# A two-layer decoder trunk on one core: where attention's and the mixer's small transposes stand in TensorE's queue

## The chip, the cores and the metric

The kernel runs on one core of one Trainium2 chip. The metric is the device time of one execution in microseconds (us), lower is better. The kernel before takes 1362.99 us, the median of three runs (1362.9 to 1364.49).

The engines named here are TensorE (PE, matrix products and transposes), VectorE (DVE), ScalarE (ACT), GpSimd (POOL) and the queue that starts most loads (SP). TensorE writes into PSUM banks; DVE and ACT read them from there.

## The reference

The program is a trunk of two layers over 512 tokens with 1024 channels, in float32:

```python
# layer 0
x = x + mamba2_mixer(x)      # 4 groups; per group: y = rms_norm(y_group) ; then y @ out_w
x = x + conv_ffn(x)
# layer 1
k, v = shared_kv(x)          # k = rms_norm per 64 channels
q = rms_norm(rms_norm(x) @ q_w)
logits = q @ k.T * scale + bias[t5_bucket(distance)]        # causal, two maps a head
attn = softmax(logits[0]) - lam * softmax(logits[1])
o = rms_norm(attn @ v) * (1 - lam_init)                      # 8 heads of 128 channels
x = x + o @ out_w
x = x + conv_ffn(x)
```

Three things in it matter here. The mixer's result is normed group by group (512 channels each) before its output projection. Keys and queries are normed after their projection. Each head's result `o` is normed over its 128 channels before the output projection, in which every one of the eight heads takes part.

## The kernel before

**Products.** Activations lie with channels on the partitions, as `xT[0..7]`, eight blocks of 128 channels by 512 tokens. Every large product is done as three passes (`mm3`, L195): high part by high part, high by low, low by high. So one block of 128 output channels over eight input blocks is 24 products of 128x128 by 128x512, and over four input blocks it is 12. Each chunk of weights is loaded by SP into a raw buffer (three), and split by ACT (`wh`, L147 or L165) and DVE (`wl`, L151 or L166) into one of three weight buffers. `chunk()` (L187) starts the loads and splits two chunks ahead of the use. Of the eight PSUM banks four are for products (`mm_bank`) and four for everything else (`aux_bank`).

**Order.** The order on each engine isn't the program's order. A planner goes through the instructions by priority, which is the place in the program, and puts each where, by its own estimate of durations, its inputs are ready. If an instruction isn't ready by that estimate, a later one that is ready goes ahead. On the chip each engine then takes its instructions in that fixed order, and waits where one isn't ready yet. `tc.issue_after(ins)` gives every instruction traced inside it, on the engine of `ins`, one more condition for the planner: it comes behind `ins`. It is no wait on the chip.

**Mixer.** For each of four groups: two blocks of products and convolutions for B and C (`conv_block`, L528), four for the values, then the scan woven with four blocks for the gate. Then the sum of squares over the group's channels (`gacc`) is turned into a factor for each token: `token_rsqrt` (L443) transposes the sums (`tr_g`, L447), reduces them and takes the inverse root by twelve small DVE instructions (L418 to L430), and `along_tokens` (L453) transposes the factor back into a row (`al_g`, L457). `normed` (L740) does both and then makes the normed high and low parts `yh`, `yl`. They are read by `out_proj` (L700), eight blocks of 12 products: for group g it comes at the end of group g + 1. In the last group three blocks of `out_proj(2)` come ahead of `normed`, and five behind it.

**Attention.** `proj` (L917) makes keys, queries or values of four heads, in four pieces of 24 products, and yields after each half piece (12 products). `qk` (L939) adds the norm over 64 channels (ACT L945 and L946, DVE L947, the inverse root, DVE L954) and turns the normed tokens by sixteen transposes (`ktk`, `ktq`, L958) into `kT` and `qT`. The position biases are a product of a small one-hot table (`ps_rb`, L907), written to DRAM (`bd`, L911) and read back per head (`tr`, L986) for the logits.

Each head has three parts of query blocks, and each part goes through four steps: `logits` (L981, products `lg` L1001, DVE L1007, exponentials L1015), `weigh` (L1018), `turn` (transposes `at`, L1033) and `values` (products `po`, L1042, copied by ACT to `ot`, L1045). `heads` (L1066) runs the steps of successive parts one round apart. When a head's last part is through, `finish` (L1048) norms it (ACT L1052, DVE L1053, inverse root, DVE L1055 on `ot`), turns it by four transposes (`oT`, L1058), and makes the high and low parts `oh` (ACT L1061) and `ol` (DVE L1062).

The heads are woven with other products: heads 0 to 3 with the value projection (`lead_in`, L464) and then with the next keys and queries (`weave`, L472, one half piece for two steps); heads 4 to 7 with their values and then with the first half of the output projection, `attn_out(0)`, one block for four steps. `attn_out(1)` follows at the end: for each of the eight blocks of output channels 12 products over heads 4 to 7 (`ps_ao`), then `add_to_stream` (L511): DVE adds the block to `xT` (L512), ACT scales the high part `xgh` (L414), DVE makes the low part `xgl` (L415), ACT squares and POOL adds (L498, L500). The first product group of the second FFN (`ps_g`) reads all eight `xgh` and `xgl`, one after the other.

Of the kernel before, what the change touches and what calls it, by code (L numbers as in the profile page):

```python
# [18 lines left out]
P = 128  # L19
# [20 lines left out]
def trunk_kernel(ctx: ExitStack, tc, x, ssm_ln_g, ssm_in_w, ssm_conv_w, ssm_conv_b, ssm_dt_bias,  # L40
# [154 lines left out]
    def mm3(ps, wh, wl, xh, xl, start, stop):  # L195
        pe.matmul(ps, wh, xh, start=start, stop=False)  # L196
        pe.matmul(ps, wh, xl, start=False, stop=False)  # L197
        pe.matmul(ps, wl, xh, start=False, stop=stop)  # L198
# [319 lines left out]
    with tc.tile_pool(name="ssm_y", bufs=1) as yp, tc.tile_pool(name="ssm", bufs=1) as sp:  # L518
        def in_block(key):
# [4 lines left out]
            for k in range(KB):  # L524
                mm3(ps, wh[:, k, :], wl[:, k, :], xgh[k], xgl[k], k == 0, k == KB - 1)
# [174 lines left out]
        def out_proj(g, yh, yl, norm):  # L700
            for c in range(4):
                wh, wl = chunk("out%d_%d" % (g, c))
                for i in range(2):
                    m = 2 * c + i
                    ps = mm_bank("ps_o%d_%d" % (g, m))
                    for k in range(4):
                        mm3(ps, wh[:, k, i * P:(i + 1) * P], wl[:, k, i * P:(i + 1) * P],
                            yh[k], yl[k], k == 0, k == 3)
# [31 lines left out]
        def normed(g, xs, acc):  # L740
            r = along_tokens(token_rsqrt(acc, sp, "g%d" % g, 512), "g%d" % g)
# [14 lines left out]
        for g in range(NG):  # L756
# [6 lines left out]
            conv_block(16 + g, "in%d" % (32 + g), bT)  # L763
            conv_block(20 + g, "in%d" % (36 + g), cT)
# [10 lines left out]
            for b in range(4):  # L775
# [5 lines left out]
                else:  # L781
                    a2 = sp.tile([P, T], F32, tag="gacc", name="gacc%d_%d" % (g, b), bufs=2)
                    (pool if b == 1 else dve).tensor_tensor(out=a2, in0=acc, in1=sq, op=ALU.add)
                    acc = a2
            if g == 0:
                params_b()
                prev = normed(g, xs, acc)
            elif g < NG - 1:
                run(out_proj(g - 1, *prev, None))
                prev = normed(g, xs, acc)  # L790
            else:
# [3 lines left out]
                prev = normed(g, xs, acc)  # L795
# [99 lines left out]
    with tc.tile_pool(name="att_o", bufs=1) as op_, tc.tile_pool(name="att", bufs=1) as ap:  # L895
        rts = []

# [3 lines left out]
        hb = NBIAS // 2  # L901
        for i in range(2):
            oh = ap.tile([32, hb], F32, tag="p0", name="oh%d" % i, bufs=3)
            bv = ap.tile([AH, hb], F32, tag="p1", name="bv%d" % i, bufs=3)
            sync.dma_start(oh, onehot[:, i * hb:(i + 1) * hb])
            ps = aux_bank("ps_rb%d" % i)
            pe.matmul(ps[:AH, :hb], rb, oh, start=True, stop=True)  # L907
            act.activation(bv, ps[:AH, :hb], AF.Copy)
            if i == 0:
                dve.memset(bv[:, 0:P - 1], NEG)  # L910
            sync.dma_start(bd[:, i * hb:(i + 1) * hb], bv)  # L911
# [5 lines left out]
        def proj(key, evac):  # L917
            pss = [mm_bank("ps_%s_%d" % (key, b)) for b in range(NT)]
            for k0 in range(0, KB, 2):
                wh, wl = chunk("%s_%d" % (key, k0))  # L920
                for b in range(NT):
                    ts = slice(b * P, (b + 1) * P)
                    for k in range(k0, k0 + 2):
# [3 lines left out]
                        pe.matmul(pss[b], xgl[k][:, ts], wh[:, k - k0, :], start=False, stop=sp_)  # L927
                    if b == 1:
                        yield
# [9 lines left out]
        def qk(key, dst, gcol):  # L939
# [12 lines left out]
            for b in range(NT):  # L952
# [3 lines left out]
                ps = aux_bank("kt%s_%d" % (key, b))  # L956
                for h in range(4):
                    pe.transpose(ps[:, h * P:(h + 1) * P], kn[b][:, h * P:(h + 1) * P], ident)  # L958
                act.activation(dst[:, :, b * P:(b + 1) * P], ps.rearrange("p (h t) -> p h t", h=4),
                               AF.Copy, scale=c2[:, gcol:gcol + 1])  # L960
# [87 lines left out]
        def finish(h, st):  # L1048
# [6 lines left out]
            dve.tensor_tensor(out=ot, in0=ot, in1=so.unsqueeze(2).to_broadcast([P, NT, P]), op=ALU.mult)  # L1055
            ps = aux_bank("oT%d" % h)
# [9 lines left out]
        def heads(hs, os):  # L1066
# [6 lines left out]
            for t in range(n + 4):  # L1073
                if t < n:
                    us[t].logits()
                    yield
# [8 lines left out]
                if 0 <= t - 4 < n and us[t - 4].part == len(PARTS) - 1:  # L1085
                    os.append(finish(us[t - 4].h, us[t - 4].st))
                    yield

        def attn_out(i, os, norm):
            for c in range(4):  # L1090
                wh, wl = chunk("ao%d_%d" % (i, c))
                for j in range(2):
                    m = 2 * c + j
                    ps = mm_bank("ps_ao%d_%d" % (i, m))
                    for k in range(4):
                        mm3(ps, wh[:, k, j * P:(j + 1) * P], wl[:, k, j * P:(j + 1) * P],
                            os[k][0], os[k][1], k == 0, k == 3)
                    add_to_stream(m, ps, 24, norm)
# [48 lines left out]
```

## Time and profile before

| | before |
|---|---|
| median of 3 runs | 1362.99 us (1362.9 to 1364.49) |
| the profiled execution | 1362.61 us |
| its span, from the first to the last instruction | 1360.5 us |
| granted TensorE clock, mean | 0.999 |
| PE busy | 1349.6 us (99%) |
| DVE, ACT, POOL busy | 912.9, 664.5, 90.8 us |
| the mixer's groups | until about 384 us of the span |
| attention, from the first key product to the last of the output projection | 744.4 to 992.3 us |

The view of the profile that counts most here is that of the waits: for each kind of instruction it sums the time that its engine stood idle ahead of it, and names what ended the idle time. The time rows give one instruction each: its start in us from the begin of the span, its duration, engine, line, operation, output and inputs, shapes and count; in brackets the idle time ahead of it and what ended it. PE's products are pipelined: the 512-column products start 0.23 us apart and are shown as 0.39 long. So a row with no bracket may still start late against the row ahead.

### The profile page before, as it was taken

To read this page: it belongs to the slowest core of one execution; us is meant where nothing else is said; L and a number is where in the kernel's file an instruction comes from. 1 tells how busy PE (TensorE), PEld (TensorE's weight loads), DVE (VectorE), ACT (ScalarE), POOL (GpSimd) and SP (SyncE) were. 2 spreads that over 40 slices of the span, in tenths; PEclk is the share of its full clock that TensorE was granted. 3 is DMA by queue.
4 is the path that set the end of the run, shared out by engine and by line. 5 is a ranking of instruction groups with operands and counts; after the bars stand their busy time and mean duration, and the time that the engine had idled before them with its cause. 6 is when DMAs were issued, how large, how long until landed. Compare 5 with 4: busy or idle time off the path is not lost.

```text
span 1360.5 us, 16900 instructions
## 1 busy us (share of the span) xinstructions
PE 1349.6 (99%) x6421; PEld 1096.7 (81%) x6421; DVE 912.9 (67%) x1528; ACT 664.5 (49%) x1090; POOL 90.8 (7%) x118
## 2 busy tenths in 40 slices
PE   9999999999999999999999999999999999999998
PEld 7878887887888888888888777777788888888887
DVE  5989778688877774367755565767777773367742
ACT  5696744652444443134434466777664443134420
POOL 4330301200010000000002000000110000000000
PEclk9999999999999999999999999999999999999999
DMA  7452433432333332333233332221223333333322
GB/s 202 144 163 78 147 109 95 146 93 70 93 93 93 95 107 93 93 95 105 88 93 104 117 86 70 78 78 56 58 82 93 96 105 94 93 96 105 94 93 78
DMA packets 179904, 135.06 MB, mean 99 GB/s; under 512 B 6508, under 2 KB 163632, under 8 KB 179824
## 3 DMA queue, kind: packets, MB, share of 16 engines
q1 hardware_dynamic: 174048, 120.84, 30.0%
q0 software_dynamic: 4496, 12.05, 2.8%
q10 hardware_dynamic: 1280, 1.10, 0.2%
q8 instruction: 50, 0.82, 0.2%
q14 instruction: 30, 0.25, 0.1%
HBM read 131.72 MB, written 2.25 MB: 98 GB/s over the span
## 4 chain that ended last, share of the span: by engine, by line
PE 90%; DVE 5%; ACT 3%; issue 1%; DMA 1%; SPq 0%; DVEq 0%; ACTq 0%
PE ps_g L197 6%; PE ps_g L198 6%; PE ps_g L196 6%; PE ps_u L196 6%; PE ps_u L198 6%; PE ps_u L197 6%; PE ps_in L197 5%; PE ps_in L198 5%; PE ps_in L196 5%; PE ps_d L848 3%; PE ps_d L196 3%; PE ps_d L198 3%; PE ps_d L847 3%; PE ps_d L846 3%; PE ps_d L197 3%; PE ps_o L198 2%
## 5 line engine op out<-in xcount | busy, mean ns | idle before, releaser
L196 PE MATMUL ps_u<-xgh,wh_u 128*128 128x512 f32 x352 | 137.5, 391 | 0.0
L197 PE MATMUL ps_g<-xgl,wh_g 128*128 128x512 f32 x352 | 137.1, 390 | 0.0
L196 PE MATMUL ps_g<-xgh,wh_g 128*128 128x512 f32 x352 | 137.1, 390 | 0.0
L198 PE MATMUL ps_u<-xgh,wl_u 128*128 128x512 f32 x352 | 137.1, 389 | 0.0
L198 PE MATMUL ps_g<-xgh,wl_g 128*128 128x512 f32 x352 | 137.1, 389 | 0.0
L197 PE MATMUL ps_u<-xgl,wh_u 128*128 128x512 f32 x352 | 137.1, 389 | 0.0
L197 PE MATMUL ps_in<-xgl,wh_in 128*128 128x512 f32 x304 | 121.0, 398 | 0.0
L196 PE MATMUL ps_in<-xgh,wh_in 128*128 128x512 f32 x304 | 120.9, 398 | 0.0
L198 PE MATMUL ps_in<-xgh,wl_in 128*128 128x512 f32 x304 | 119.6, 394 | 0.0
L151 DVE TENSOR_TENSOR wl_d<-wr_d,wh_d 128x1024 fp32r<-128x1024 f32 (+1 forms) x46 | 54.2, 1179 | 96.9 <-ACT wh_d L147 96.7
L147 ACT ACTIVATE wh_d<-wr_d 128x1024 fp32r<-128x1024 f32 (+1 forms) x46 | 47.1, 1024 | 130.3 <-PE ps_d L848 62.4
L870 ACT ACTIVATE hh<-vg 128x512 fp32r<-128x512 f32 x44 | 27.8, 632 | 114.9 <-DVE vg L869 114.9
L818 DVE TENSOR_TENSOR uu<-ps_u,nr_f 128x512 f32<-128x512 f32 x44 | 30.4, 692 | 78.0 <-PE ps_u L198 77.9
L197 PEld LDWEIGHTS ps_g<-xgl,wh_g 128*128 128x128 f32 x352 | 66.1, 188 | 13.9 <-DVE xgl L415 0.3
L198 PEld LDWEIGHTS ps_u<-xgh,wl_u 128*128 128x128 f32 x352 | 66.1, 188 | 13.8
L198 PEld LDWEIGHTS ps_g<-xgh,wl_g 128*128 128x128 f32 x352 | 66.1, 188 | 13.7
L196 PEld LDWEIGHTS ps_g<-xgh,wh_g 128*128 128x128 f32 x352 | 66.1, 188 | 13.6
L197 PEld LDWEIGHTS ps_u<-xgl,wh_u 128*128 128x128 f32 x352 | 66.1, 188 | 13.6
L196 PEld LDWEIGHTS ps_u<-xgh,wh_u 128*128 128x128 f32 x352 | 66.1, 188 | 13.5
L147 ACT ACTIVATE wh_g<-wr_g 128x1024 fp32r<-128x1024 f32 x44 | 46.7, 1061 | 51.7 <-PE ps_u L197 32.3
L865 ACT ACTIVATE vg<-vg 128x512 f32<-128x512 f32 x44 | 27.8, 632 | 84.4 <-DVE vg L821 84.4
L846 PE MATMUL ps_d<-wh_d,hh 128*128 128x512 f32 x176 | 68.5, 389 | 0.0
(349 smaller groups left out, 3228.3 us busy)
## 6 DMA issues: line engine op xcount, KB each, us to landing
wr_g<-in_ffn_up_w_dram SPq DMA_DIRECT2D x44, 512.0 KB, 3.9
wr_u<-in_ffn_up_w_dram SPq DMA_DIRECT2D x44, 512.0 KB, 3.9
wr_d<-in_ffn_down_w_dram SPq DMA_DIRECT2D x42, 512.0 KB, 3.6
wr_in<-in_ssm_in_w_dram SPq DMA_DIRECT2D x40, 512.0 KB, 3.9
m<-cumd POOLq DMA_DIRECT2D x16, 512.0 KB, 4.5
wr_out<-in_ssm_out_w_dram SPq DMA_DIRECT2D x16, 512.0 KB, 3.5
wr_k<-in_kv_w_dram SPq DMA_DIRECT2D x8, 512.0 KB, 4.0
wr_q<-in_q_w_dram SPq DMA_DIRECT2D x8, 512.0 KB, 4.1
```

Of the source, the lines that this page charges most:

```text
L147: return act.activation(self.wh[:, :self.n], self.raw[:, :self.n], AF.Copy)
L151: return dve.tensor_tensor(out=self.wl[:, :self.n], in0=self.raw[:, :self.n], in1=self.wh[:, :self.n].bitcast(F32), op=ALU.subtract)
L196: pe.matmul(ps, wh, xh, start=start, stop=False)
L197: pe.matmul(ps, wh, xl, start=False, stop=False)
L198: pe.matmul(ps, wl, xh, start=False, stop=stop)
L818: dve.tensor_tensor(out=u, in0=ps, in1=r, op=ALU.mult)
L846: pe.matmul(pss[b], hh[k][:, ts], wh[:, k - k0, :], start=k == 0, stop=False)
L847: pe.matmul(pss[b], hh[k][:, ts], wl[:, k - k0, :], start=False, stop=False)
L848: pe.matmul(pss[b], hl[k][:, ts], wh[:, k - k0, :], start=False, stop=k == n - 1)
L865: act.activation(ga, ga, AF.Silu)
L870: act.activation(h, ga, AF.Copy)
```

## The change

Five edits, which share one device: `mm3` returns its last product, and `state["last"]` holds the last large product that was traced.

- The mixer: the factor is computed where it was, but `along_tokens` and the normed parts come behind the first convolution block of the next group (24 products), and are put behind its last product. In the last group they come two blocks of `out_proj(2)` later, behind the fifth of eight.
- Attention gets a list `pend`. What is on it is traced at the next call of `pended()`, behind `state["last"]`. Such calls stand in `proj` after the first half of each piece, at the head of each round of `heads`, and in the last output projection.
- The transposes of keys and queries (`turned`), and those of the normed head with `oh` and `ol` (`turned_out`), are put on that list; the norm itself stays where it was.
- The bias rows are put on the list after the fourth half piece of `k0`, and so come behind its 60th product; the one-hot table's loads stay first.
- The first half piece of each value projection is traced ahead of the heads that it is woven with, so that the queries' transposes have products to stand behind. The weave of the heads with the other products is thereby shifted by one half piece.
- `attn_out(1)` does the first five blocks (m0 to m4) in two goes: nine products over heads 4 to 6 first, the three over head 7 later. Head 7's transposes come behind the nine products of m3. Then come nine of m4, the three last ones of m0 to m4 with their additions, and m5 to m7 as before. The block m4 has a bank of the other four.

```diff
         pe.matmul(ps, wh, xl, start=False, stop=False)
-        pe.matmul(ps, wl, xh, start=False, stop=stop)
+        return pe.matmul(ps, wl, xh, start=False, stop=stop).ins
...
             for k in range(KB):
-                mm3(ps, wh[:, k, :], wl[:, k, :], xgh[k], xgl[k], k == 0, k == KB - 1)
+                state["last"] = mm3(ps, wh[:, k, :], wl[:, k, :], xgh[k], xgl[k], k == 0, k == KB - 1)
             return ps
...
                     for k in range(4):
-                        mm3(ps, wh[:, k, i * P:(i + 1) * P], wl[:, k, i * P:(i + 1) * P],
-                            yh[k], yl[k], k == 0, k == 3)
+                        state["last"] = mm3(ps, wh[:, k, i * P:(i + 1) * P], wl[:, k, i * P:(i + 1) * P],
+                                            yh[k], yl[k], k == 0, k == 3)
                     add_to_stream(m, ps, 16, norm)
...
-        def normed(g, xs, acc):
-            r = along_tokens(token_rsqrt(acc, sp, "g%d" % g, 512), "g%d" % g)
+        def normed(g, xs, rt):
+            with tc.issue_after(state["last"]):
+                r = along_tokens(rt, "g%d" % g)
             yh, yl = [], []
...
             conv_block(16 + g, "in%d" % (32 + g), bT)
+            if g:
+                prev = normed(*todo)
             conv_block(20 + g, "in%d" % (36 + g), cT)
...
                     acc = a2
+            factor = lambda: token_rsqrt(acc, sp, "g%d" % g, 512)
             if g == 0:
                 params_b()
-                prev = normed(g, xs, acc)
+                todo = g, xs, factor()
             elif g < NG - 1:
                 run(out_proj(g - 1, *prev, None))
-                prev = normed(g, xs, acc)
+                todo = g, xs, factor()
             else:
...
                     next(op)
-                prev = normed(g, xs, acc)
+                rt = factor()
+                for _ in range(2):
+                    next(op)
+                prev = normed(g, xs, rt)
                 run(op)
...
         rts = []
+        pend = []
+        def pended():
+            with tc.issue_after(state["last"]):
+                for f in pend:
+                    f()
+            pend.clear()
...
         hb = NBIAS // 2
+        ohs = []
         for i in range(2):
-            oh = ap.tile([32, hb], F32, tag="p0", name="oh%d" % i, bufs=3)
-            bv = ap.tile([AH, hb], F32, tag="p1", name="bv%d" % i, bufs=3)
-            sync.dma_start(oh, onehot[:, i * hb:(i + 1) * hb])
-            ps = aux_bank("ps_rb%d" % i)
-            pe.matmul(ps[:AH, :hb], rb, oh, start=True, stop=True)
-            act.activation(bv, ps[:AH, :hb], AF.Copy)
-            if i == 0:
-                dve.memset(bv[:, 0:P - 1], NEG)
-            sync.dma_start(bd[:, i * hb:(i + 1) * hb], bv)
+            ohs.append(ap.tile([32, hb], F32, tag="p0", name="oh%d" % i, bufs=3))
+            sync.dma_start(ohs[i], onehot[:, i * hb:(i + 1) * hb])
+        def bias_rows():
+            for i in range(2):
+                bv = ap.tile([AH, hb], F32, tag="p1", name="bv%d" % i, bufs=3)
+                ps = aux_bank("ps_rb%d" % i)
+                pe.matmul(ps[:AH, :hb], rb, ohs[i], start=True, stop=True)
+                act.activation(bv, ps[:AH, :hb], AF.Copy)
+                if i == 0:
+                    dve.memset(bv[:, 0:P - 1], NEG)
+                sync.dma_start(bd[:, i * hb:(i + 1) * hb], bv)
...
                         pe.matmul(pss[b], xgh[k][:, ts], wl[:, k - k0, :], start=False, stop=False)
-                        pe.matmul(pss[b], xgl[k][:, ts], wh[:, k - k0, :], start=False, stop=sp_)
+                        state["last"] = pe.matmul(pss[b], xgl[k][:, ts], wh[:, k - k0, :],
+                                                  start=False, stop=sp_).ins
                     if b == 1:
+                        pended()
                         yield
...
                                   op=ALU.mult)
-                ps = aux_bank("kt%s_%d" % (key, b))
-                for h in range(4):
-                    pe.transpose(ps[:, h * P:(h + 1) * P], kn[b][:, h * P:(h + 1) * P], ident)
-                act.activation(dst[:, :, b * P:(b + 1) * P], ps.rearrange("p (h t) -> p h t", h=4),
-                               AF.Copy, scale=c2[:, gcol:gcol + 1])
+            def turned():
+                for b in range(NT):
+                    ps = aux_bank("kt%s_%d" % (key, b))
+                    for h in range(4):
+                        pe.transpose(ps[:, h * P:(h + 1) * P], kn[b][:, h * P:(h + 1) * P], ident)
+                    act.activation(dst[:, :, b * P:(b + 1) * P], ps.rearrange("p (h t) -> p h t", h=4),
+                                   AF.Copy, scale=c2[:, gcol:gcol + 1])
+            pend.append(turned)
             yield
...
-        def finish(h, st):
+        def normed_out(h, st):
             ot = st["ot"]
...
             dve.tensor_tensor(out=ot, in0=ot, in1=so.unsqueeze(2).to_broadcast([P, NT, P]), op=ALU.mult)
+        def turned_out(h, st):
+            ot = st["ot"]
             ps = aux_bank("oT%d" % h)
...
             for t in range(n + 4):
+                pended()
                 if t < n:
...
                 if 0 <= t - 4 < n and us[t - 4].part == len(PARTS) - 1:
-                    os.append(finish(us[t - 4].h, us[t - 4].st))
+                    normed_out(us[t - 4].h, us[t - 4].st)
+                    pend.append(lambda u=us[t - 4]: os.append(turned_out(u.h, u.st)))
                     yield
...
         def attn_out(i, os, norm):
+            held = []
             for c in range(4):
                 wh, wl = chunk("ao%d_%d" % (i, c))
-                for j in range(2):
-                    m = 2 * c + j
-                    ps = mm_bank("ps_ao%d_%d" % (i, m))
-                    for k in range(4):
-                        mm3(ps, wh[:, k, j * P:(j + 1) * P], wl[:, k, j * P:(j + 1) * P],
-                            os[k][0], os[k][1], k == 0, k == 3)
-                    add_to_stream(m, ps, 24, norm)
-                    yield
-        run(qk("k0", kT[0], 48))
-        run(qk("q0", qT[0], 49))
+                late = (2, 2, 1, 0)[c] if i else 0
+                pss = [(aux_bank if c == 2 and j < late else mm_bank)("ps_ao%d_%d" % (i, 2 * c + j))
+                       for j in range(2)]
+                def part(j, ks, c=c, wh=wh, wl=wl, pss=pss):
+                    for k in ks:
+                        state["last"] = mm3(pss[j], wh[:, k, j * P:(j + 1) * P], wl[:, k, j * P:(j + 1) * P],
+                                            os[k][0], os[k][1], k == 0, k == 3)
+                    if 3 in ks:
+                        add_to_stream(2 * c + j, pss[j], 24, norm)
+                        yield
+                for j in range(late):
+                    run(part(j, range(3)))
+                    held.append(part(j, (3,)))
+                if late and c == 1:
+                    pended()
+                if c == 2:
+                    yield from chain(*held)
+                for j in range(late, 2):
+                    yield from part(j, range(4))
+        ops = chain(qk("k0", kT[0], 48), qk("q0", qT[0], 49))
+        for _ in range(4):
+            next(ops)
+        pend.append(bias_rows)
+        run(ops)
         os0, os1 = [], []
-        lead_in(hs := heads(range(0, 4), os0), vproj("v0", 0), 2)
+        next(vp := vproj("v0", 0))
+        lead_in(hs := heads(range(0, 4), os0), vp, 2)
         weave(hs, chain(qk("k1", kT[1], 48), qk("q1", qT[1], 49)), 1, 2)
-        lead_in(hs := heads(range(4, 8), os1), vproj("v1", 1), 2)
+        next(vp := vproj("v1", 1))
+        lead_in(hs := heads(range(4, 8), os1), vp, 2)
         weave(hs, attn_out(0, os0, None), 1, 4)
```

## The prediction

> **What bounds the kernel now.** I read the page first, then the waits of TensorE (PE), then the time rows round each wait that an edit touches.
>
> ```profile
> PE 1349.6 (99%) x6421; PEld 1096.7 (81%) x6421; DVE 912.9 (67%) x1528; ACT 664.5 (49%) x1090; POOL 90.8 (7%) x118
> PE 90%; DVE 5%; ACT 3%; issue 1%; DMA 1%; SPq 0%; DVEq 0%; ACTq 0%
> ```
>
> PE is busy for 99% of the span and carries 90% of the chain that ended last. No product is removed, so the change can only win what PE waits, and a refill behind each wait. The view of waits, for PE alone, in us in total, times and longest:
>
> ```profile
> PE oT L1058 <- DVE ot L1055: 3.1, 5, 1.1
> ...
> PE al_g L457 <- DVE tr_g L430: 0.6, 2, 0.3
> ...
> PE ktk L958 <- DVE knk L954: 0.3, 1, 0.3
> PE ps_rb L907 <- DMA oh<-onehot_dram: 0.3, 1, 0.3
> ...
> PE ktq L958 <- DVE knq L954: 0.2, 1, 0.2
> ```
>
> The edits aim at these 4.5 us in ten waits. Each waiting instruction is a small transpose or product, and PE takes matmuls in the order of its queue, so the big products behind it stand too.
>
> **1. The mixer's factor rows (al_g).** Time rows of PE round the wait in group 1:
>
> ```profile
> 178.27 0.40 PE L198 MATMUL ps_o<-yh,wl_out 128*128 128x512 f32 x1
> 178.50 0.38 PE L447 MATMUL tr_g<-ident,gacc 128*128 128x128 f32 x2
> ...
> 182.83 0.39 PE L198 MATMUL ps_in<-xgh,wl_in 128*128 128x512 f32 x1
> 183.53 0.62 PE L457 MATMUL al_g<-ident,tr_g 128*128 128x128 f32 x4 [0.32 <-DVE tr_g L430]
> ```
>
> Without a wait a transpose starts 0.23 us behind the product ahead of it (178.27 to 178.50); here it took 0.70. So a wait costs its idle time and about 0.16 us more, 0.48 in all. The chain of DVE behind tr_g lasts 5.0 us (178.50 to 183.53). Now al_g stands behind all 24 products of the next group's first block, 24 x 0.23 = 5.4 us, after four tr_g transposes (0.36, an estimate from two in 0.38 with overlap): it starts at 5.8, and 0.8 us are to spare. Two such waits (the row gives 0.6 in 2): gain **0.95**. If DVE were later by more than 0.8, it would come back. The normed tiles are read by a projection a whole group later, so their delay of about 0.8 us reaches nobody. In the last group two more blocks of products stand ahead of it; no wait is listed there, and I count nothing.
>
> **2. The bias rows (ps_rb).**
>
> ```profile
> 744.36 0.39 PE L925 MATMUL ps_k<-wh_k,xgh 128*128 128x512 f32 x1
> ...
> 747.76 0.39 PE L925 MATMUL ps_k<-wh_k,xgh 128*128 128x512 f32 x1
> 748.40 1.23 PE L907 MATMUL ps_rb<-oh,rb 32*8 32x320 f32 x4 [0.25 <-DMA oh<-onehot_dram]
> ...
> 800.60 1.80 PE L1001 MATMUL lg<-kT,qT 64*128 64x128 f32 x12
> ```
>
> From 747.76 to 748.40 are 0.64, against 0.23: 0.41. Behind 60 products of k0 instead of 16 the four matmuls run at about 744.4 + 13.6 = 758.0, and the DMA has long landed. The two writes of bd on SP and the reads of tr behind them move by about 10 us; their first user, logits, is at 800.60, so 30 us hide them. The weight loads queued behind them on SP are fetched two chunks ahead. Gain **0.41**.
>
> **3. Keys, queries, heads 0 to 6.** A transpose put "behind a later product" has only a lower bound: the planner places an instruction where it holds it ready, and it did so before.
>
> ```profile
> 768.30 0.39 PE L925 MATMUL ps_q<-wh_q,xgh 128*128 128x512 f32 x1
> ...
> 773.51 0.39 PE L927 MATMUL ps_q<-wh_q,xgl 128*128 128x512 f32 x1
> 773.97 0.66 PE L958 MATMUL ktk<-ident,knk 128*128 128x128 f32 x4
> ```
>
> The keys already stand behind 24 products of q0 (768.30 to 773.51 is 5.2 us); the new bound is 12, so it binds nothing. The heads:
>
> ```profile
> 927.83 1.06 PE L1042 MATMUL po<-vt,at 128*128 128x128 f32 x8
> ...
> 931.58 0.93 PE L1001 MATMUL lg<-kT,qT 64*128 64x128 f32 x8
> ...
> 933.41 0.48 PE L196 MATMUL ps_ao<-oh,wh_ao 128*128 128x512 f32 x1
> ...
> 936.48 0.39 PE L197 MATMUL ps_ao<-ol,wh_ao 128*128 128x512 f32 x1
> 937.80 0.41 PE L1058 MATMUL oT<-ident,ot 128*128 128x128 f32 x2 [0.93 <-DVE ot L1055]
> ...
> 954.91 0.41 PE L1058 MATMUL oT<-ident,ot 128*128 128x128 f32 x2 [1.07 <-DVE ot L1055]
> ...
> 967.08 0.41 PE L1058 MATMUL oT<-ident,ot 128*128 128x128 f32 x2 [0.66 <-DVE ot L1055]
> ```
>
> From 933.41 to 936.48 lie 14 products: all of block m2 and two of m3, and then oT of head 4 waits 0.93. The new bound is "behind m2", which the old order meets. Heads 5 and 6 are alike (bounds m4 and m7). With head 3 (3.1 less these three and head 7's 0.18 leaves about 0.23), the keys (0.3, and 0.07 at 773.97) and the queries (0.2) these are seven waits of 3.5 us idle, 4.6 with 0.16 for each. They can all go, because every step of the weave is shifted by half a step; or none, since the placing by readiness stays. I hold the second as nearer, as the rows show the bound met already, and count one wait in seven as lost by the shift: gain **0.65**, ends 0 and 4.6 (the other end is rival C).
>
> **4. The last head.** Rows of ACT, PE and DVE:
>
> ```profile
> 970.16 0.28 ACT L1045 ACTIVATE ot<-po 128x128 f32<-128x128 f32 x1 [1.04 <-PE po L1042]
> ...
> 973.39 0.39 PE L198 MATMUL ps_ao<-oh,wl_ao 128*128 128x512 f32 x1
> 973.96 0.63 PE L1058 MATMUL oT<-ident,ot 128*128 128x128 f32 x4 [0.18 <-DVE ot L1055]
> ...
> 975.35 0.75 DVE L1062 SCALAR_TENSOR_TENSOR ol<-oT,c,oh 128x512 fp32r<-128x512 f32 x1 [1.54 <-ACT oh L1061]
> ```
>
> The chain from 970.16 to the transpose is 3.8 us; 36 products of blocks m0 to m3 (8.2 us) now cover it. From the transpose's start to the end of ol are 2.1 us; four transposes (0.4) and nine products of m4 (2.0) cover that by 0.3. Gain 0.57 - 0.23 = **0.34**.
>
> Its price lies behind it. Five blocks now end within 15 products (3.4 us), and all additions come late. Groups of DVE instructions from the first addition to the last low part, and the rows at both ends:
>
> ```profile
> L415 DVE SCALAR_TENSOR_TENSOR xgl<-xT,c,xgh 128x512 fp32r<-128x512 f32 x8 | 7.9, 1005 | 1.6 <-ACT xgh L414 1.6
> L512 DVE TENSOR_TENSOR xT<-ps_ao,xT 128x512 f32<-128x512 f32 x8 | 5.4, 684 | 1.0 <-PE ps_ao L198 0.9
> L151 DVE TENSOR_TENSOR wl_g<-wr_g,wh_g 128x1024 fp32r<-128x1024 f32 x2 | 2.8, 1386 | 0.3 <-ACT wh_g L147 0.2
> L151 DVE TENSOR_TENSOR wl_u<-wr_u,wh_u 128x1024 fp32r<-128x1024 f32 x1 | 1.5, 1536 | 0.1
> L151 DVE TENSOR_TENSOR wl_ao<-wr_ao,wh_ao 128x1024 fp32r<-128x1024 f32 x1 | 1.2, 1226 | 0.0
> ```
> ```profile
> 977.04 1.29 DVE L512 TENSOR_TENSOR xT<-ps_ao,xT 128x512 f32<-128x512 f32 x2 [0.94 <-PE ps_ao L198]
> ...
> 992.26 0.39 PE L196 MATMUL ps_g<-xgh,wh_g 128*128 128x512 f32 x1
> ...
> 997.26 0.50 PE L197 MATMUL ps_g<-xgl,wh_g 128*128 128x512 f32 x1
> ```
>
> Call S the first product of the FFN (992.26). PE asks for the last xgl at S + 5.0 (997.26); its row is long, so it came just in time. DVE began at S - 15.2 and had 20.2 us. In the new order the first block ends 48 products ahead of S, so DVE begins at S - 10.7 and has 15.7 us. Its work before the last xgl, with three splits (two of them wait for the weight buffers that the held blocks keep) at 1.2, 1.4 and 1.5, is 7.9 + 5.4 + 4.1 = 17.4: 1.7 us too much. With xgl at 0.75, as ol, of like form, has it, it is 15.5 and fits. Ends 0 and, at the old pace of 20.2, 4.5; I take **0.8 lost**, half of 1.7.
>
> The Trainium skill, "Perfetto Trace Analysis", section "Optimizing Tensor Performance" (Matmuls), says that independent groups of matmuls should rotate through PSUM banks so that the evacuation of one overlaps the products of the next. It speaks against five groups that end together; by it all of this tail counts, 1.7 instead of 0.8, and the sum would be 0.65 us gain. The rows rather show that three blocks of products (36 x 0.23 = 8.3 us) still follow, and the fifth bank's owner, m5, begins 12 products after m0's last, 2.7 us against an addition of 0.7.
>
> **The sum**, against the profiled execution (1362.61 us, span 1360.5; the median of the runs is 1362.99, 0.4 above): 0.95 + 0.41 + 0.65 + 0.34 - 0.8 = 1.55 us gain, from the median **1361.4 us**.
>
> **Rivals.**
>
> A. All waits go and the tail hides: 0.95 + 0.41 + 4.6 + 0.34 = 6.3, so 1356.7; with the tail's 0.8 it is 1357.5. For it: the half step by which products now run ahead of the heads. Against it: the bounds that were met before.
>
> B. Slower, by the tail: DVE keeps its old pace from the later start, the last xgl is ready at S - 10.7 + 20.2 = S + 9.5, PE waits 4.5 us in the first FFN product group, and no wait of part 3 goes: 1362.99 - 1.7 + 4.5 = 1365.8. It decides where DVE has more than 15.7 us of work ahead of the last xgl. For it: 18.8 us of DVE work (the groups above) in the 20.2 us before. Against it: with five additions ready at once DVE needn't sit out the 1.6 us for xgh.
>
> C. The planner puts oT of heads 4 to 6 directly behind their bound. Head 4's chain from the values' end to its transpose is 8.9 us (927.83 + 1.06 to 937.80); cover is then logits, turns and values (1.8, 931.58 to 933.41) and m2 (2.7): a wait of 4.4 instead of 0.93, 3.5 lost for each such head. Two of them: 1362.99 - 1.7 + 7.0 = 1368.3. Against it: the keys, put 24 products late.
>
> D. It does nothing: the order was planned by readiness, the waits go elsewhere, 1363.0.
>
> **How the numbers follow.** Chances: my forecast 0.42, A 0.33, B 0.11, C 0.04, D 0.10. The forecast's own range is 1360.0 to 1362.9 (tail 0 to 1.7, two waits more or none). The range reaches to A with the tail, less a little, and to B: 1357.3 to 1365.4. About 0.2% (2.7 us, 1360.3 and 1365.7) is what a measurement of this kernel tells from no change. Faster: A and a tenth of the forecast, 0.36. Slower: C and most of B, 0.12. Within: 0.52.
>
> **What would show it.** Right: no wait at al_g, ps_rb and head 7's oT; oT of heads 4 to 6 still waits for ot, 0.5 to 1 us each; DVE busy without a gap from S - 11 to S + 5 and a wait for xgl of about 1 us in the first FFN products. Wrong: oT's total wait below 1 us (A), a wait for xgl over 3 us (B), waits at oT over 3 us (C), or al_g and ps_rb gone with the same span (D).

## The result, and the profile after

The changed kernel takes 1372.65 us (median of six runs, 1371.7 to 1373.56) against 1363.2 us (1362.9 to 1364.94) of the kernel before on the same chip. The ratio is 1.0066 with an interval of 1.0053 to 1.0079: 9.45 us slower. The profiled execution took 1372.77 us, its span 1370.4 us, 9.9 more than before.

The view of TensorE's waits of the kernel after (what waits, for whom, us in total, times, longest). The lines of attention stand some 20 to 30 further down than before: `oT` is now L1088, `ktk` L983.

```profile
PE ps_g L197 <- DVE xgl L415: 4.2, 2, 2.2
PE oT L1088 <- DVE ot L1082: 2.9, 5, 0.9
PE ktk L983 <- DVE knk L976: 2.2, 2, 1.4
...
PE ps_g L196 <- ACT xgh L414: 0.6, 1, 0.6
```

The waits at `al_g`, at `ps_rb` and at head 7's `oT` are gone, as intended. A wait of 4.2 us for `xgl` is new, the keys wait 2.2 us where they waited 0.3, and the sum at `oT` is nearly what it was (2.9 against 3.1).

Where the time went shows in the starts of the same product in both traces, after less before: first product of the keys -0.2 us, first of the queries -0.5, first of the values +0.8 (the keys' transposes lie between), first product of the second FFN (S) +2.4, transposes of the FFN's norm (`tr_nf`) +8.9, end +9.9. So three places lose: the keys 1.3, the heads 1.6, and the seam between the output projection and the FFN 7.5. The waits of the heads' stretch, from the values to S, sum to 3.9 us after and 3.5 before, so most of the 1.6 shows as no listed wait, and its cause stays open in part. Time rows of PE at that seam, after; before, the same stretch from S to `tr_nf` went from 992.26 to 997.95 with no wait:

```profile
994.69 0.39 PE L196 MATMUL ps_g<-xgh,wh_g 128*128 128x512 f32 x1
...
1000.53 0.50 PE L197 MATMUL ps_g<-xgl,wh_g 128*128 128x512 f32 x1 [2.05 <-DVE xgl L415]
...
1001.89 0.49 PE L196 MATMUL ps_g<-xgh,wh_g 128*128 128x512 f32 x1 [0.62 <-ACT xgh L414]
...
1004.54 0.80 PE L197 MATMUL ps_g<-xgl,wh_g 128*128 128x512 f32 x1 [2.15 <-DVE xgl L415]
1005.13 0.63 PE L198 MATMUL ps_g<-xgh,wl_g 128*128 128x512 f32 x1
1005.55 0.63 PE L196 MATMUL ps_g<-xgh,wh_g 128*128 128x512 f32 x1
...
1006.83 1.06 PE L447 MATMUL tr_nf<-ident,nacc_f 128*128 128x128 f32 x4
```

From S to `tr_nf` are 12.1 us instead of 5.7, with 4.8 us of waits. The rest is in the rows behind the last wait: the products start 0.42 us apart (1005.13 to 1005.55) instead of 0.23. I come back to that at the end.

What VectorE does from the first addition (984.01) to the end of the last low part is called the tail here. Its groups (us in total, mean ns of one, idle time ahead), after:

```profile
L415 DVE SCALAR_TENSOR_TENSOR xgl<-xT,c,xgh 128x512 fp32r<-128x512 f32 x8 | 10.7, 1365 | 0.1
L512 DVE TENSOR_TENSOR xT<-ps_ao,xT 128x512 f32<-128x512 f32 x8 | 5.2, 682 | 1.3 <-PE ps_ao L198 1.3
L151 DVE TENSOR_TENSOR wl_g<-wr_g,wh_g 128x1024 fp32r<-128x1024 f32 x2 | 2.4, 1218 | 0.0
L151 DVE TENSOR_TENSOR wl_u<-wr_u,wh_u 128x1024 fp32r<-128x1024 f32 x1 | 2.3, 2314 | 0.0
L151 DVE TENSOR_TENSOR wl_ao<-wr_ao,wh_ao 128x1024 fp32r<-128x1024 f32 x1 | 1.2, 1217 | 0.0
```

VectorE is idle there for 0.1 us, and its mean `xgl` grew from 1005 to 1365 ns. The same tile's own view gives the smallest, median and largest duration; first before, then after:

```profile
L415 DVE SCALAR_TENSOR_TENSOR xgl<-xT,c,xgh x8: 740/749/1783, 979.5 to 996.5; 128x512 fp32r<-128x512 f32 x8
```
```profile
L415 DVE SCALAR_TENSOR_TENSOR xgl<-xT,c,xgh x8: 735/1688/1793, 988.3 to 1004.4; 128x512 fp32r<-128x512 f32 x8
```

An `xgl` lasts either 0.75 us or 1.7 to 1.8. Before, two of eight were long, now five. The long ones lie beside GpSimd's additions of squares (`nacc`):

```profile
988.26 4.15 DVE L415 SCALAR_TENSOR_TENSOR xgl<-xT,c,xgh 128x512 fp32r<-128x512 f32 x3
```
```profile
988.81 3.05 POOL L500 TENSOR_TENSOR nacc_f<-nacc_f,nsq_f 128x512 f32<-128x512 f32 x2 [241.31 <-ACT nsq_f L498]
```

### The profile page after: what moved, and what is told of

It reads as the page before. It is cut to its first block, busy times and chain, and to the rows that moved or that the text cites. A ratio compares the mean times of both kernels' runs of the same rounds, so it can differ in the third digit from the quotient of the medians.

```text
span 1370.4 us, 16900 instructions
## 1 busy us (share of the span) xinstructions
PE 1353.1 (99%) x6421; PEld 1097.7 (80%) x6421; DVE 918.8 (67%) x1528; ACT 664.5 (48%) x1090; POOL 91.2 (7%) x118
## 4 chain that ended last, share of the span: by engine, by line
PE 90%; DVE 5%; ACT 3%; issue 1%; DMA 1%; SPq 0%; DVEq 0%; ACTq 0%
PE ps_g L197 6%; PE ps_g L198 6%; PE ps_u L196 6%; PE ps_u L197 6%; PE ps_u L198 6%; PE ps_g L196 6%; PE ps_in L197 5%; PE ps_in L198 5%; PE ps_in L196 5%; PE ps_d L855 3%; PE ps_d L197 3%; PE ps_d L196 3%; PE ps_d L854 3%; PE ps_d L853 3%; PE ps_d L198 3%; PE ps_o L198 2%
## 5 line engine op out<-in xcount | busy, mean ns | idle before, releaser
L196 PE MATMUL ps_d<-hh,wh_d 128*128 128x512 f32 x176 | 68.5, 389 | 0.0
```

## The experiments

The theory after the first look had three causes: the tail on VectorE, the bias rows, and something in the turned heads. First came the four parts of the change, each alone on the kernel before. All kernels were timed in five rounds beside the kernel before (1362.8 to 1363.1 us).

**1. The mixer's edit alone.**

```
+ if g: prev = normed(*todo)        # behind the next group's first block; al_g with issue_after(last product)
```

> The kernel before with the mixer's edit alone (factor rows behind the next group's first block). If the prediction's term holds: both waits at al_g go, 0.95 us faster than before, 1362.2. Rival, from the profile after: the two waits go (0.98 us by the starts of the products behind them), but group 0 loses 0.6 and the first block of the FFN 0.4 again, so 0.2 us faster or nothing. If the part is the same as in the whole change, the first product of the keys' projection starts at 744.2 instead of 744.36.

Measured 1361.79 us, ratio 0.9992 (0.9983 to 1.0001). The waits at `al_g` are gone, and the keys' first product starts at 743.33 instead of 744.36: 1.0 us, near the predicted term. In the whole change it stood only 0.2 us earlier: there 0.6 us were lost ahead of the first `al_g`, where the edit touches nothing (a wait of 0.36 for `m` at 73.20 that the trace before doesn't have is part of it), and 0.4 in the first block of the first FFN, which this run doesn't show. One trace alone is uncertain by as much as the term: that product starts at 744.07 to 744.79 in the eight traces of kernels without this edit, and at 742.55 to 744.52 in the six with it. The means are 0.9 apart.

**2. The bias rows alone.**

```
+ for _ in range(4): next(ops)      # 48 products of the keys
+ pend.append(bias_rows)
```

> The kernel before with the bias rows' move alone. The prediction: 0.4 us faster. Rival, from the profile after: the copy of the biases (tb) on VectorE waits for a DMA that now leaves 10 us later, the keys' sums of squares stand behind it on the same queue, and the transposes of the keys wait 1.0 to 1.4 us; gain 0.3 less 1.3, so 0.8 to 1.0 us slower, with ktk the longest wait of TensorE between 770 and 780. If the keys' wait comes from their own pended transposes instead, it is absent here and the run is 0.4 us faster.

Measured 1365.76 us, ratio 1.0016 (1.0007 to 1.0025), 2.2 us slower by the ratio. Time rows of VectorE and PE in this run:

```profile
768.81 0.69 DVE L962 TENSOR_REDUCE ssk<-ksqk 128x8 f32<-128x512 f32 x1 [0.76 <-ACT ksqk L961]
771.58 0.43 DVE L1007 COPY tb<-tr 128x512 f32<-128x512 f32 x1 [2.08 <-DMA tr<-bd]
771.92 0.74 DVE L166 SCALAR_TENSOR_TENSOR wl_q<-wr_q,c,wh_q 128x512 fp32r<-128x512 f32 x1
772.59 0.68 DVE L962 TENSOR_REDUCE ssk<-ksqk 128x8 f32<-128x512 f32 x1
...
776.00 1.32 PE L976 MATMUL ktk<-ident,knk 128*128 128x128 f32 x8 [1.99 <-DVE knk L969]
```

The second head's copy `tb` stands in VectorE's order ahead of the keys' last sum of squares. It waits 2.08 us for its load, and the sum, whose input ACT had written at 770.49, waits with it until 772.59; at the end PE waits 1.99 us. In the kernel before, `tb` was through at 761.3 and that sum started at 770.55. The keys were not turned late by any pending here, so the rows' move alone is the cause. From the start of the queries to that of the values this costs 1.8 us, and 0.3 are gained ahead of it. The ratio says more than this 1.5, and more than the 0.8 to 1.0 expected. The eleven times lie in two groups, five of 1363.56 to 1364.54 us (the profiled run is one of them) with a mean granted clock of 1.000, and six of 1365.76 to 1366.93 with 0.999. So TensorE's clock may have fallen behind this wait in the second group; no trace of that group is there to show it.

**3. The rows 24 products earlier,** on top of the mixer's edit: put on the list after 24 products of the keys, they run behind the 36th instead of the 60th.

```
- for _ in range(4): next(ops)
+ for _ in range(2): next(ops)
```

> The mixer's edit, and the bias rows behind 24 products of the keys instead of 48. If the copy of the biases in VectorE's queue was what made the keys late: the copies now run before the keys' sums of squares, the wait at ktk is below 0.3 us, and the gain of 0.3 to 0.4 stays: 1361.4, 0.4 faster than the mixer's edit alone. If any move of the rows makes the keys late: a wait of 1 to 2 us at ktk and 1363.5.

Measured 1361.6 us, ratio 0.9992 (0.9982 to 1.0001).

```profile
759.93 0.43 DVE L1014 COPY tb<-tr 128x512 f32<-128x512 f32 x1 [0.24 <-DMA tr<-bd]
765.00 0.42 DVE L1014 COPY tb<-tr 128x512 f32<-128x512 f32 x1
765.66 0.69 DVE L969 TENSOR_REDUCE ssk<-ksqk 128x8 f32<-128x512 f32 x1 [0.24 <-ACT ksqk L968]
```

Both copies now run ahead of the first sum, the waits at `ktk` are 0.3 in all as before, and `ps_rb` (753.24) waits for nothing. It is not the move that costs but where the copy's load lands. The 0.4 us expected beside the mixer's gain are not resolved: 1361.6 against 1361.79.

**4. Keys, queries and heads turned later, alone** (with the values' first half ahead of the heads, without held blocks).

> The kernel before with keys, queries and heads (the last one too) turned behind a later product and the values' first half ahead, without the last head's held blocks. The prediction: 0.65 to 1 us faster. From the profile after: the waits at head 0 (0.79) and the keys of the second half (0.79 against 0.25) cost 1.5 us, heads 4 to 6 give 0.8 back, so 0.5 to 1 us slower; and the first wait at the keys (1.4 in the whole change) is 0.1 or less, since the bias rows stand where they stood. If the pending itself makes the keys late, that wait is over 1 us here and the run 2 us slower.

Measured 1369.38 us, ratio 1.0046 (1.0034 to 1.0059): much worse than either number. Ahead of S it is as read from the whole change: the keys of the second half wait 0.8 us, the first keys don't, and S is 1.6 us late. But 4 more are lost behind S, without a held block:

```profile
981.83 1.29 DVE L512 TENSOR_TENSOR xT<-ps_ao,xT 128x512 f32<-128x512 f32 x2 [0.95 <-PE ps_ao L198]
...
999.43 2.42 DVE L415 SCALAR_TENSOR_TENSOR xgl<-xT,c,xgh 128x512 fp32r<-128x512 f32 x2
```
```profile
993.87 0.39 PE L196 MATMUL ps_g<-xgh,wh_g 128*128 128x512 f32 x1
...
1003.54 1.01 PE L447 MATMUL tr_nf<-ident,nacc_f 128*128 128x128 f32 x4
```

The first addition comes 12.0 us ahead of S, not 15.2. So a fourth theory: the 12 products of the values that run ahead (2.7 us) push the heads back against the stream of products, and the tail with them. Two runs tell the parts of this edit apart.

**5. The same without the values ahead.**

```
- next(vp := vproj("v0", 0)); lead_in(hs := heads(range(0, 4), os0), vp, 2)     # and v1
+ lead_in(hs := heads(range(0, 4), os0), vproj("v0", 0), 2)
```

> Keys, queries and heads turned behind a later product, as in the run with that part alone, but without the first half of the values' products ahead of the heads. In that run the first addition of the tail came 12.0 us ahead of the FFN's first product, against 15.2 before: 3.2 us, near the 2.7 us of the 12 products moved ahead. If the move is the cause: the addition is 15 us ahead again, the first block of the FFN takes 5.7 us, and the run is 1363 to 1364.5 instead of 1369.4. If the turned outputs behind later products are: it stays above 1367.

Measured 1363.59 us, ratio 1.0002 (0.9993 to 1.0011). The first addition is at 977.18, S at 992.39 (15.2 apart), and the waits at `oT` are 3.1 us in five, as before. Turning behind a later product does nothing that this measurement can tell, neither good nor bad.

**6. Only the second half's values ahead.**

```
- lead_in(hs := heads(range(4, 8), os1), vproj("v1", 1), 2)
+ next(vp := vproj("v1", 1)); lead_in(hs := heads(range(4, 8), os1), vp, 2)
```

> The kernel before with one edit: the first 12 products of the values' second half run ahead of heads 4 to 7. If each product that runs ahead of the heads brings the FFN nearer and leaves the tail on VectorE where it was: the first addition is 12 to 12.5 us ahead of the FFN's first product, the first block of the FFN takes 9 to 10 us instead of 5.7, and the run is 1365.5 to 1367. If the move is harmless: 1362.8, and the loss of the turned part lies in its later turns.

Measured 1367.18 us, ratio 1.0029 (1.0018 to 1.0039). Twelve products in another place, and nothing else, cost 4 us.

```profile
980.61 1.29 DVE L512 TENSOR_TENSOR xT<-ps_ao,xT 128x512 f32<-128x512 f32 x2 [0.96 <-PE ps_ao L198]
```
```profile
1000.02 0.80 PE L197 MATMUL ps_g<-xgl,wh_g 128*128 128x512 f32 x1 [2.15 <-DVE xgl L415]
...
1002.33 0.96 PE L447 MATMUL tr_nf<-ident,nacc_f 128*128 128x128 f32 x4
```

S stands where it stood (0.4 later, as all of this trace from the mixer on), the heads' waits are even 0.8 us shorter (2.3), and the first addition is 3.6 us later. What is left of the turned part, 2.2 us between this run and run 4, is by difference the first half's values ahead, with the waits at head 0 and at the second keys (0.8 each); no run has that part alone.

**7. The last head's part alone** (five held blocks, nothing else).

> The kernel before with the last head's part last, alone: five blocks of the output projection held. The prediction: 0.5 us slower (0.34 gained, 0.8 lost). From the profile after, where the first product group of the FFN takes 12.1 us instead of 5.7: 6 us slower, 1369, VectorE without a gap from the first addition to the last low part, 21 us. If the slow tail of the whole change came from its heads being late as well, it is 3 us or less here.

Measured 1369.35 us, ratio 1.0044 (1.003 to 1.0058). Head 7's wait is gone (S is 0.5 us earlier against the start of this trace), and from S (992.07) to `tr_nf` (1004.22) it takes 12.15 us, against 12.14 in the whole change. Heads that are late as well add nothing there, because the held blocks alone fix how many products follow the first addition.

**8. The same without GpSimd's sums.** This kernel leaves out six of the seven additions behind the norm of the second FFN; the squares on ACT stay.

```
+ if self.name == "f1" and k < KB - 1: return      # ahead of the addition of squares
```

> The kernel with the last head's part alone (five held blocks), and the sum of squares of the last attention stream without its six additions on GpSimd (so the norm of the second FFN is wrong: that part of the computation is left out). In that kernel an xgl beside a GpSimd addition takes 1.77 us, alone 0.75; six of eight xgl and one weight split are so hit, about 7 us of VectorE's 21. If it is this contention that makes the tail too long: VectorE needs 14 us of the 15.7 it has, the waits for xgl go, and the run is 0 to 0.5 us faster than before, 1362.5 to 1363. If the late start alone does it, whatever VectorE's instructions last: 1369 stays.

Measured 1361.68 us, ratio 0.9993 (0.9984 to 1.0002). VectorE's groups from the first addition on, in this run:

```profile
L415 DVE SCALAR_TENSOR_TENSOR xgl<-xT,c,xgh 128x512 fp32r<-128x512 f32 x8 | 5.7, 745 | 0.1
L514 DVE TENSOR_TENSOR xT<-ps_ao,xT 128x512 f32<-128x512 f32 x8 | 5.2, 684 | 1.3 <-PE ps_ao L198 1.3
...
L151 DVE TENSOR_TENSOR wl_u<-wr_u,wh_u 128x1024 fp32r<-128x1024 f32 x1 | 1.2, 1217 | 0.0
```

All `xgl` last 0.75 (in run 7 five of the eight were long, not the six of the expectation), the split 1.2 instead of 2.3, the tail 15.05 us instead of 21.14, and no wait is left in the first block (5.45 us from S to `tr_nf`). The late start costs nothing by itself; the six GpSimd additions beside VectorE are what makes the tail too long for it.

**9. Three held blocks instead of five.**

```
- late = (2, 2, 1, 0)[c] if i else 0
+ late = (2, 1, 0, 0)[c] if i else 0
```

> The last head's part alone, with three held blocks instead of five. If the loss is how late VectorE is (its 20 to 21 us from the first addition against the distance of that addition from the first product of the FFN plus 5.0 us): the first addition comes 12.5 to 13 us ahead of that product instead of 10.7, and the run is 1365.5 to 1367, half of the loss of five. If holding at all is what costs (a bank, a weight buffer): 1369 as with five.

Measured 1365.72 us, ratio 1.002 (1.0011 to 1.0028): half the loss, with the first addition 13.2 us ahead of S.

The traces of these runs, and of run 10 below, make one table. The times are the starts of VectorE's first addition and of S, the end of the last `xgl` and the start of `tr_nf`, all from time rows, in us; the last three columns are their differences.

| kernel | first addition | S | last `xgl` ends | S less first addition | last `xgl` behind S | `tr_nf` behind S |
|---|---|---|---|---|---|---|
| before | 977.04 | 992.26 | 997.21 | 15.2 | 4.95 | 5.7 |
| turned, values not ahead (5) | 977.18 | 992.39 | 997.34 | 15.2 | 4.95 | 5.7 |
| five held, no sums (8) | 981.33 | 992.00 | 996.38 | 10.7 | 4.4 | 5.45 |
| heads two steps later (10) | 975.72 | 991.41 | 997.20 | 15.7 | 5.8 | 6.5 |
| three held (9) | 978.75 | 991.92 | 999.16 | 13.2 | 7.2 | 8.0 |
| v1 ahead (6) | 980.61 | 992.65 | 1000.64 | 12.0 | 8.0 | 9.7 |
| turned (4) | 981.83 | 993.87 | 1001.85 | 12.0 | 8.0 | 9.7 |
| five held (7) | 981.39 | 992.07 | 1002.53 | 10.7 | 10.5 | 12.15 |
| after | 984.01 | 994.69 | 1005.14 | 10.7 | 10.5 | 12.14 |

With the sums on GpSimd VectorE needs 20.0 to 21.5 us wherever it starts. So each microsecond by which the first addition comes nearer to S makes the last `xgl` about a microsecond later behind S, and with five held blocks the tail itself is 1 us longer. Where the waits are long, another 1 us passes between the last `xgl` and `tr_nf` (1.7 instead of 0.75): that is the clock, told at the end. The kernel before had no slack at all there (4.95 against the 5.0 at which PE asks).

**10. The heads' turns two steps later,** with the mixer's edit.

```
+ due.append((t + 2, lambda u=us[t - 4]: os.append(turned_out(u.h, u.st))))
```

> The mixer's edit, and the turned outputs of heads 0 to 6 two steps of the weave later instead of one, with the keys, the queries, the values and the last head as before. If one step was too little because the chain to the turn lasts 4 to 7 us: the waits at oT fall from 3.1 to below 0.5, and the run is 2.5 to 3.4 us faster than the mixer's edit alone, 1358.5 to 1359.3. If the planner's order puts the wait elsewhere (head 7, the tail on VectorE): 1361.8 or slower, with a wait for xgl in the first block of the FFN.

Measured 1361.7 us, ratio 0.9994 (0.9985 to 1.0003): no gain over the mixer's edit, where 2.5 to 3.4 us were expected. The waits at `oT` do go, and others come for part of them (`po` 0.5, `at` 0.8 in two kinds, `oT` 0.7 in two kinds). From the first product of the values to S the heads have gained 0.6 us on run 1. Then PE waits 0.7 us for `xgl`: the tail begins 1.1 us earlier against that product, but takes 21.5 us and ends 0.2 later than in run 1, so what was gained ahead of S was lost behind it. Why the tail takes longer there, no run isolates.

**11. A version that also clears the tail.** Mixer, rows as in run 3, heads two steps later, and the squares' sums on VectorE behind the last `xgl`.

```
- (dve if k == KB - 1 else pool).tensor_tensor(out=self.acc, in0=self.acc, in1=sq, op=ALU.add)
+ with tc.issue_after(state["low"]):               # the last xgl
+     for s in self.sqs: dve.tensor_tensor(out=self.acc, in0=self.acc, in1=s, op=ALU.add)
```

> The mixer's edit, the bias rows behind 24 products, the heads' turns two steps later, and the last attention stream's sum of squares on VectorE behind all its low parts instead of on GpSimd beside them. The heads' later turns alone gained 0.6 us by the FFN's first product and lost it again to a wait for xgl. If VectorE's tail is what took it: no wait for xgl (15 us of work instead of 20), the sums end before the transposes of the FFN's norm ask for them, and the run is 1360.3 to 1361.3. If the sums are then late themselves: a wait at tr_nf and 1362 or more.

Measured 1360.7 us, ratio 0.9985 (0.9976 to 0.9994): faster than both kernels. (Its interval still overlaps that of the mixer's edit alone.) `xgl` again lasts 0.75 us each (746 ns mean), the last one ends 3.0 us behind S, and there is no wait for it. The sums put `tr_nf` behind 15 products of the next block and it waits 0.1 there.

**12. The whole change with the three causes undone** (no held blocks, no values ahead, rows as in run 3).

> The whole change with three things undone: the five held blocks, the 12 values' products ahead of the heads, and the bias rows 24 products earlier. If these three are all that costs: the mixer's gain of about 1.1 us is left, the rows' 0.3 beside it, the turned parts give or take 0.5 as they did alone, so 1361 to 1362.5, and no wait over 1.2 us in attention or at the FFN's first products. If the parts cost something together that none costs alone: above 1363.5.

Measured 1361.61 us, ratio 0.9992 (0.9983 to 1.0001). So nothing else in the change costs anything that this measurement can tell. The parts alone sum to more than the whole (-1.1 + 2.2 + 6.3 + 6.0 = 13.4 by the ratios, against 9.0), because runs 4 and 7 each pay for a late tail and the whole change pays for it once: leaving out the 4 us that run 4 loses behind S makes 9.4.

## Why the prediction was wrong, step by step

The step that failed most is the fourth: the price of the tail, put at 0.8 us, was 7.5. Two smaller ones failed in steps 2 and 3.

**1. The mixer's factor rows** were right: 0.95 predicted, 1.0 in the trace of run 1, 0.9 between the means of the traces with and without the edit. The 24 products cover VectorE's chain.

**2. The bias rows.** The step was right for PE: from the queries' start 0.3 us are gained. It failed at "their first user, logits, is at 800.60, so 30 us hide them". The first user is the copy `tb` on VectorE, and it isn't hidden by being early: it stands in a queue where the keys' sums are behind it. Cost 1.3 us in the whole change, 1.8 in run 2. These are its rows after:

```profile
770.44 0.43 DVE L1014 COPY tb<-tr 128x512 f32<-128x512 f32 x1 [1.52 <-DMA tr<-bd]
...
771.45 0.68 DVE L969 TENSOR_REDUCE ssk<-ksqk 128x8 f32<-128x512 f32 x1
...
774.86 1.32 PE L983 MATMUL ktk<-ident,knk 128*128 128x128 f32 x8 [1.43 <-DVE knk L976]
```

**3. Keys, queries, heads.** That bounds already met bind nothing was right: run 5 is at 1.0002, the step's end of 0. The step that failed is the one not taken. I read the values' first half ahead of the heads as the "half step" that speaks for rival A, and never followed it into VectorE's tail. Run 6 prices it at 4 us for the second half alone. In the whole change these 4 us don't come on top, because the held blocks bring the first addition to S - 10.7 in any case; there the heads lose 1.6 us, where the step counted 0.65 as gained.

**4. The last head.** The lead was right to the hundredth: S - 10.7 predicted, 10.68 measured. So was, nearly, its gain (0.5 against 0.34). The term that was mis-sized is VectorE's work: "17.4: 1.7 us too much", with a way to make it 15.5. It was 21.1. Four splits lie ahead of the last `xgl`, not three (2.4 + 2.3 + 1.2 is 5.9, against 4.1 in the sum), and five `xgl` and a split run beside GpSimd (all `xgl` 10.7, against 7.9 in the sum). The mean of 1005 ns that I took was a mix of six at 0.75 and two at 1.78; the 0.75 of `ol` was the price without GpSimd, and run 8 shows it holds for all eight when GpSimd is quiet. Held blocks come out in threes and twos, so ACT squares them in a row and GpSimd adds them in a row, just when VectorE makes the low parts.

The Trainium skill, "SBUF — State Buffer", section "Who interferes with whom", states the rule that decides this: a VectorE instruction with two SBUF inputs contends with a GpSimd instruction that reads SBUF, and one with at most one SBUF input doesn't. The traces agree: `xgl` (both inputs in SBUF) goes from 0.75 to 1.77 us and the split from 1.2 to 2.3, while the additions to `xT`, with one input in PSUM, last 0.68 beside a GpSimd addition too (the additions at 985.96, 988.10 and 994.20 of the kernel before meet one; these rows show the second). The prediction didn't use it. The rule that it did weigh, on rotating banks, pointed the right way, but no row shows PE waiting for a bank: it waits for `xgl`.

```profile
988.06 1.30 POOL L500 TENSOR_TENSOR nacc_f<-nacc_f,nsq_f 128x512 f32<-128x512 f32 x1 [0.86 <-ACT nsq_f L498]
```
```profile
988.10 0.68 DVE L512 TENSOR_TENSOR xT<-ps_ao,xT 128x512 f32<-128x512 f32 x1
```

**Rivals.** B was the one that came: its mechanism, old pace from a later start, its place, its order of work. Its price of 4.5 became 5.5 of lateness for the last `xgl` (10.5 less 4.95 behind S) and about 2 for the clock, told below. It had a chance of 0.11; the argument against it, that VectorE needn't sit out 1.6 us for `xgh`, was true (idle 0.1) and outweighed by GpSimd. C didn't come: heads 4 to 6 wait 0.49, 0.45 and 0.92. A didn't come: the waits at `oT` are nearly what they were. D holds for run 5 alone. B's time, 1365.8, counted the gains of steps 1, 2 and 4 in full and nothing for the keys and the heads.

The sum against 9.9 us of span: -0.5 up to the queries, 1.3 at the keys, 1.6 at the heads, 7.5 behind S.

## What to carry to other kernels

A tail that ends just in time has a second price list: whatever brings its consumer nearer, or its producer later, counts there in full, and a gain ahead of the consumer is kept only if the tail's end moves with it, as with the mixer's edit and not in run 10. So ask of each moved product where it leaves the engine that follows. And before a mean duration is used, look at its smallest, median and largest: two clusters mean two situations, and the change may move instructions from one to the other. A copy that waits for a load is hidden only if nothing urgent stands behind it on its engine.

## What the runs showed of the hardware that I had not expected

TensorE's clock fell behind the waits. Windows of the kernel after (stretch, length, then busy us and count of PE, PEld, DVE, ACT and POOL, granted clock, DMA share, GB/s):

```profile
995.00:1000.00 5.00, 3.48 (x16) 2.54 (x14) 5.00 (x3) 2.62 (x4) 4.77 (x3) 1.00 0.00 1
1000.00:1004.00 4.00, 1.23 (x3) 0.48 (x3) 4.00 (x5) 2.38 (x4) 1.43 (x1) 0.85 0.46 132
1004.00:1008.00 4.00, 3.46 (x10) 2.90 (x11) 1.82 (x4) 1.06 (x1) 0.00 (x0) 0.50 0.43 128
1008.00:1013.00 5.00, 5.00 (x21) 4.00 (x21) 3.65 (x14) 0.00 (x0) 0.00 (x0) 0.84 0.36 104
1013.00:1020.00 7.00, 7.00 (x34) 5.75 (x33) 5.25 (x7) 4.19 (x5) 0.00 (x0) 1.00 0.25 74
```

There are three waits within some 6 us, the longest 2.15, with three products between them, and the granted clock falls to 0.50. By windows of one microsecond (0.89 from 1002 to 1003, 0.69 from 1009 to 1010, 0.50 between them, 1.00 outside) it is at half from about 1002.8 to 1009.6: 6.8 us, of which 5 lie behind the last wait. Nine products and four transposes take 4.9 us there (1004.54 to 1009.40; soon behind, the products are 0.23 apart again) instead of about 2.5: more than 2 us beyond the waits themselves. The same reckoning gives 6.8 us at half in run 7, and 3.4 in runs 4, 6 and 9, so in these traces the half clock comes in pieces of 3.4 us. A single wait of 1.99 us in the trace of run 2 left the clock at 1.00; two of 0.6 and 1.1 close together in run 9 left 0.67 over the next 4 us. No run here varied the waits for this alone, so where the bound lies stays open. The Trainium skill, "TensorE: Matmul & The Clock Gate", section "What's actually happening", says that the clock goes to half after an idle window of about 3.4 us and returns after a busy one; the half agrees with these rows, and so does the length, once or twice 3.4 us; but the fall came here without any single wait that long, behind waits with a few products between them.
